# Two-layer streaming encoder on one core: sums of squares on GpSimd, halved last units, a late quarter turned ahead, and diagonal products in the last norm

## The chip, the cores and the metric

The kernel runs on one core of one Trainium2 chip. The metric is the device time of one execution in microseconds (us). The runs shown are three executions; a further execution was taken with the hardware profiler, and all rows come from that one.

A core has TensorE (PE; its weight loads are listed as PEld), VectorE (DVE), ScalarE (ACT), GpSimd (POOL) and SyncE (SP, which here issues nearly all transfers). TensorE's clock has two levels, 2.4 and 1.2 GHz; the profile gives the granted clock as a share of the higher one, so 0.50 is 1.2 GHz.

## The reference

One sequence of 256 tokens and 2048 channels goes through two layers, all in float32. With `mod = silu(c) @ w_mod + b_mod` cut into shift_m, scale_m, gate_m, shift_f, scale_f and gate_f, each layer computes:

```python
h = layer_norm(x) * (1 + scale_m) + shift_m
uv, q_c, kv_c, k_r, sb, sc, sh, ag = split(h @ w_in)
y_b = mla(rms_norm(q_c) @ w_uq, rms_norm(kv_c) @ w_ukv, k_r)
y = concat(y_a, y_b, y_c, y_d) @ w_out
x = layer_norm(ALPHA * x + (1 + gate_m) * y, g, b)
h = layer_norm(x) * (1 + scale_f) + shift_f
gate, val = split(h @ w_up)
x = layer_norm(ALPHA * x + (1 + gate_f) * ((silu(conv3(gate)) * val) @ w_down), g, b)
```

y_a is a chunked gMLP, y_c a short gated convolution, y_d a convolution of width 31 with its own norm. The latent attention y_b needs the sum of squares over 384 columns of q_c and over 256 columns of kv_c for each token. A product keeps float32 precision by one of two routes: "exact" float32 products, which the profile shows as two records each, or a split of each operand into a high and a low part, with three products hi*hi, lo*hi and hi*lo.

## The kernel before

The residual x stays on the core in two token tiles of 128 rows (t = 0 and 1). Weights are streamed. `weights` (L423) loads 1 MB into a ring of four raw tiles and makes the two parts, ScalarE the cast (L458), VectorE the difference (L459). `stream` (L402) is the order of all work: it issues a load, flushes the products appended before (`pending`), appends this load's products, and calls `pump`. So the products of one load stand in TensorE's program behind the next load. The order of instructions on one engine is fixed when the program is built, by a planner that may put ready work ahead of work that is not.

**The modulation in the background.** `mod_stream` (L324) is a generator: each of its units loads a piece of w_mod into the same raw ring and accumulates it on VectorE (`mod_step` L245, lines L249 and L251). `pump` (L376) adds the phase's rate (RATES, L35) to a credit and draws one unit for each whole credit. `settle` (L300) turns a finished accumulator into the modulation's columns with small products into ps_mod, a copy, and ScalarE's or VectorE's step on it. Of layer 0's SHIFT_F and SCALE_F the last quarter (k tiles 12 to 15, LATE_KT) is held back: four times one unit of each, eight units, drawn by the phase `first` (six loads) and, what is left, by `needs` in `late`.

**The first group of the feed-forward.** `first_group` (L616) makes the first 512 columns of `h @ w_up` with exact weights, quarter by quarter as the norm's k tiles become ready. `to_hT` (L587) normalises a quarter of one token tile (xn, ScalarE), turns it by four transposes on TensorE (L597) into one PSUM bank and applies scale and shift from there (ScalarE for t = 0, VectorE L608 for t = 1). In layer 0 three quarters are done at once; the fourth, `rest` (L655), waits for the held-back modulation. `ffn_up` (L1366) runs six other loads in the meantime (gv 0, gg 0, gv 1, gg 1, gv 2, gg 2) and puts `late` (L1401) behind them: needs, rest, gated_first.

**The output projections.** `out_proj` (L666) serves o (w_out) and d (w_down) in both layers, so o0, d0, o1, d1. The last 512 columns keep their last four loads back (`tail`) and then take token tile 0's products first, tile 1's second. `finish_bank` (L699) reads the PSUM bank: yg (L704), x (L707), batch statistics (L710). Then comes the norm: `second` (L729) for tile 0 where another layer part follows, `norm` (L770) otherwise: two VectorE passes per 512 columns, L777 (centre and gain) and L780 (rstd and bias); at the program's end (then is None) a store of each quarter (L784), 256 KB.

**The attention.** `mix_b` (L1028) squares five blocks of 128 x 256 on ScalarE (L1050), scales q (L1054) and sums the squares over the partitions with products against ones into ps_ss: ten products, 20 records. From these come rr (`power`, GpSimd, L114), diagonal tiles dgB and ps_rkv. The C products (C_c) of the same projection stand around them.

## Time and profile before

| what | before |
|---|---|
| runs, us | 2276.4, 2278.2, 2282.6 (median 2278.2) |
| profiled execution, its own time | 2274.61 us |
| its span | 2272.8 us |
| TensorE busy | 2229.4 us (98%) |
| VectorE busy | 1780.5 us (78%) |
| ScalarE busy | 1107.0 us (49%) |
| GpSimd busy | 35.1 us (2%) |
| memory traffic | 605.19 MB, mean 266 GB/s |

The span runs from the first to the last instruction of the profiled execution; its own time is 1.8 us more. All starts below are us from the span's start. Records of TensorE overlap, and their ends are modelled, so the cost of a run of products is read from start to start. "[0.52 <-PE ps_xT L597]" behind a row means that its engine idled 0.52 us before it, and what released it.

### The profile page before, as it was taken

How to read it: one execution, taken by the hardware profiler on the slowest of the kernel's cores; microseconds unless marked ns; L12 is line 12 of the kernel's file. 1: busy time of each engine (PE TensorE's matmuls, PEld its weight loads, DVE VectorE, ACT ScalarE, POOL GpSimd, SP SyncE). 2: the span in 40 equal slices, each digit the busy share in tenths (PEclk: the TensorE clock that was granted, in tenths of full speed). 3: DMA queues.
4: the chain of work that ended last, by engine and by line, in shares of the span. 5: the costliest groups of instructions: out<-in, count | busy, mean ns of one | idle time of the engine just before them, and what ended most of it. 6: DMA issues, size and time to landing. Idle time of an engine off the chain costs nothing.

```text
span 2272.8 us, 31376 instructions
## 1 busy us (share of the span) xinstructions
PE 2229.4 (98%) x12311; PEld 1919.6 (84%) x12311; DVE 1780.5 (78%) x2195; ACT 1107.0 (49%) x1652; POOL 35.1 (2%) x65
## 2 busy tenths in 40 slices
PE   7999999999999999999999999999999999999998
PEld 5788886788888888888789999889888888888886
DVE  5778988878888888989977899887775565565776
ACT  3356642354455444544554434545544454454553
POOL 0011000000000000000000000000000000000000
PEclk9999999999999999999999999999999999999999
DMA  9999699778888888899867677775675555555554
GB/s 350 388 371 361 254 327 360 245 275 315 310 313 313 309 317 325 300 343 328 296 235 251 203 242 248 281 269 178 232 258 185 190 187 198 185 187 197 187 188 148
DMA packets 228717, 605.19 MB, mean 266 GB/s; under 512 B 14661, under 2 KB 27189, under 8 KB 210901
## 3 DMA queue, kind: packets, MB, share of 16 engines
q1 hardware_dynamic: 227784, 602.30, 74.2%
q8 instruction: 96, 1.57, 0.3%
q0 software_dynamic: 784, 0.90, 0.1%
q14 instruction: 53, 0.43, 0.0%
HBM read 601.05 MB, written 2.10 MB: 265 GB/s over the span
## 4 chain that ended last, share of the span: by engine, by line
PE 89%; DVE 6%; DMA 2%; issue 1%; ACT 1%; POOL 0%; SPq 0%; DVEq 0%; ACTq 0%; POOLq 0%
PE g_c L83 22%; PE v_c L83 22%; PE d L83 19%; PE o L83 7%; PE C_c L83 4%; PE D_c L83 4%; PE B_c L83 2%; DVE wlo L459 1%; PE U_c L83 1%; PE E L83 1%; PE E_c L83 1%; PE U L83 1%; PE V L83 1%; DMA wmod<-in_w_mod_dram 1%; DVE macc L251 1%
## 5 line engine op out<-in xcount | busy, mean ns | idle before, releaser
L458 ACT CAST whi<-wraw 128x1024 fp32r<-128x1024 f32 (+1 forms) x632 | 643.3, 1043 | 751.6 <-PE g_c L83 221.7
L459 DVE TENSOR_TENSOR wlo<-wraw,whi 128x1024 fp32r<-128x1024 f32 (+1 forms) x632 | 750.3, 1213 | 302.7 <-ACT whi L458 283.1
L83 PE MATMUL d<-whi,a 128*128 128x512 f32 x1344 | 388.5, 390 | 2.3 <-ACT whi L458 2.3
L251 DVE SCALAR_TENSOR_TENSOR macc<-wmod,cact,macc 128x2048 f32<-128x2048 f32 (+2 forms) x174 | 353.7, 2033 | 24.4 <-DMA wmod<-in_w_mod_dram 23.7
L83 PE MATMUL v_c<-hT,whi 128*128 128x512 f32 (+1 forms) x1456 | 343.1, 383 | 0.0
L83 PE MATMUL g_c<-hT,whi 128*128 128x512 f32 (+1 forms) x1344 | 313.3, 380 | 0.0
L83 PEld LDWEIGHTS v_c<-hT,whi 128*128 128x128 f32 x1456 | 264.5, 189 | 48.5
L83 PEld LDWEIGHTS d<-whi,a 128*128 128x128 f32 x1344 | 251.7, 188 | 55.7 <-ACT whi L458 3.5
L83 PEld LDWEIGHTS g_c<-hT,whi 128*128 128x128 f32 x1344 | 243.4, 189 | 43.2
L83 PE MATMUL d<-wlo,a 128*128 128x512 f32 x672 | 233.5, 390 | 1.7 <-DVE wlo L459 1.7
L83 PE MATMUL v_c<-hT,wlo 128*128 128x256 f32 x1400 | 190.7, 283 | 0.0
L83 PEld LDWEIGHTS v_c<-hT,wlo 128*128 128x128 f32 x1400 | 183.1, 191 | 6.6
L83 PE MATMUL g_c<-hT,wlo 128*128 128x256 f32 x1280 | 175.8, 283 | 0.0
L83 PEld LDWEIGHTS g_c<-hT,wlo 128*128 128x128 f32 x1280 | 168.2, 191 | 5.9
L83 PEld LDWEIGHTS d<-wlo,a 128*128 128x128 f32 x672 | 126.1, 188 | 30.5 <-DVE wlo L459 4.3
L478 ACT CAST a<-g 128x512 fp32r<-128x512 f32 x132 | 80.7, 619 | 81.9 <-PE d L83 80.2
L83 PE MATMUL o<-whi,a 128*128 128x512 f32 x384 | 110.5, 392 | 0.5 <-ACT whi L458 0.5
L479 DVE TENSOR_TENSOR a<-g,a 128x512 fp32r<-128x512 f32 x132 | 87.5, 683 | 5.4 <-ACT a L478 5.4
L251 DVE SCALAR_TENSOR_TENSOR qacc<-wmod,cact,qacc 128x1024 f32<-128x1024 f32 (+1 forms) x75 | 80.3, 1071 | 11.6 <-DMA wmod<-in_w_mod_dram 9.2
L83 PEld LDWEIGHTS o<-whi,a 128*128 128x128 f32 x384 | 72.0, 188 | 16.9 <-ACT whi L458 1.3
L83 PE MATMUL D_c<-hT,whi 128*128 128x256 f32 x432 | 83.0, 292 | 2.2 <-ACT hT L478 1.6
L1381 DVE SCALAR_TENSOR_TENSOR u<-g,pf,u 128x254 f32<-128x254 f32 (+1 forms) x176 | 73.5, 478 | 0.0
(370 smaller groups left out, 2618.1 us busy)
## 6 DMA issues: line engine op xcount, KB each, us to landing
wraw<-in_ffn_w_up_dram SPq DMA_DIRECT2D x168, 1024.0 KB, 4.9
wmod<-in_w_mod_dram SPq DMA_DIRECT2D x134, 1024.0 KB, 6.0
wraw<-in_ffn_w_down_dram SPq DMA_DIRECT2D x88, 1024.0 KB, 5.3
wraw<-in_w_in_dram SPq DMA_DIRECT2D x33, 1024.0 KB, 7.5
wmod<-in_w_mod_dram SPq DMA_DIRECT2D x64, 512.0 KB, 9.2
wraw<-in_w_out_dram SPq DMA_DIRECT2D x26, 1024.0 KB, 5.2
wmod<-in_w_mod_dram SPq DMA_DIRECT2D x32, 768.0 KB, 8.0
wexact<-in_w_in_dram SPq DMA_DIRECT2D x46, 512.0 KB, 7.4
```

Source lines behind the costliest of these rows:

```text
L83: pe.matmul(o, lhsT, rhs, start=start, stop=stop, skip_group_check=True)
L251: i = dve.scalar_tensor_tensor(out=acc, in0=w, scalar=col, in1=acc, op0=ALU.mult, op1=ALU.add)
L458: act.copy(hi[:, :m], r)
L459: i = dve.tensor_tensor(out=lo[:, :m], in0=r, in1=hi[:, :m].bitcast(F32), op=ALU.subtract)
L478: act.copy(hi, src)
L479: dve.tensor_tensor(out=lo, in0=src, in1=hi.bitcast(F32), op=ALU.subtract)
L1381: dve.scalar_tensor_tensor(out=u[:, sh:], in0=x[:, : S - sh], scalar=col(k, j), in1=u[:, sh:], op0=ALU.mult, op1=ALU.add)
```

## The change

It has five parts.

1. RATES: `first` is 1.335 instead of 1.2.
2. The late quarter: `mod_stream` settles SHIFT_F as soon as its last unit is drawn. `first_group` returns two more functions: `scaled` makes the normalised last quarter of both token tiles (xn), `turn_raw` transposes it and copies it into hF without scale and shift. `ffn_up` appends them behind gv 1 and gg 1. `rest` then applies scale and shift in place, two of four blocks on ScalarE and two on VectorE, and runs the products.
3. In `out_proj` the products of the last load are made in two column halves for the token tile whose norm comes first (tile 0; tile 1 at the end of the program), and `finish` takes yg and x in the same halves.
4. At the program's end `last_rows` takes the place of `norm` for token tile 1: for quarters 0 and 1 the second pass becomes a product of a diagonal tile (rstd) with x on top of the bias in PSUM, and a ScalarE copy; quarters 2 and 3 keep VectorE's two passes.
5. In `mix_b` GpSimd adds the squares (three adds of 128 x 256), so that four products, eight records, are left.

```diff
-    dict(B=1.634, C=1.9, out=1.7, first=1.2, up=0.68, down=0.83),
+    dict(B=1.634, C=1.9, out=1.7, first=1.335, up=0.68, down=0.83),
...
                             late.append((0, v, acc, LATE_KT, KT))
+                            if v == SHIFT_F:
+                                settle(len(late) - 1)
...
+        def scaled():
+            for t in range(2):
+                raw[t] = tmp_tile("xn")
+                ident_act(raw[t], X[t][:, 3 * 512 :], r[t][:, 0:1], r[t][:, 1:2])
+
+        def turn_raw():
+            for t in range(2):
+                ps = ms_tile("ps_xT")
+                for j in range(4):
+                    pe.transpose(ps[:, j * P : (j + 1) * P], raw[t][:, j * P : (j + 1) * P], ident)
+                act.copy(hF[3][:, :, t * P : (t + 1) * P], ps.rearrange("p (j t) -> p j t", j=4))
+
         def rest():
-            for q in range(quarters, 4):
-                for t in range(2):
-                    turned(t, q)
-                products(q, 0, S, False, q == 3)
-                splits(q)
...
+            for j in range(4):
+                h, sc, sh = hF[3][:, j, :], MOD[(l, m_scale, 12 + j)], MOD[(l, m_shift, 12 + j)]
+                if j % 2 == 0:
+                    ident_act(h, h, sc, sh)
+                else:
+                    dve.tensor_scalar(out=h, in0=h, scalar1=sc, scalar2=sh, op0=ALU.mult, op1=ALU.add)
+            products(3, 0, S, False, True)
+            splits(3)
...
+        first_ready = 1 if then is None else 0
+
+        def halved(t, item, ps, h):
+            parts, acts = item
+            cols = slice(h * 256, (h + 1) * 256)
+            for k, (hi, lo) in enumerate(parts):
+                ahi, alo = acts[k]
+                end = k == len(parts) - 1
+                pairs = [(ahi, hi)] if lo is None else [(ahi, hi), (ahi, lo), (alo, hi)]
+                for i, (x, y) in enumerate(pairs):
+                    mm(ps[t][0][:, cols], x[:, t * P : (t + 1) * P], y[:, cols], False, end and i == len(pairs) - 1)
...
         def finish(t, ps, c0):
+            if t == first_ready:
+                for h in range(2):
+                    y = tmp_tile("yg")[:, :256]
+                    lo = c0 + h * 256
+                    xs = X[t][:, lo : lo + 256]
+                    dve.tensor_tensor(
+                        out=y, in0=ps[t][0][:, h * 256 : (h + 1) * 256], in1=box["gate"][:, lo : lo + 256], op=ALU.mult
+                    )
+                    dve.scalar_tensor_tensor(out=xs, in0=xs, scalar=ALPHA, in1=y, op0=ALU.mult, op1=ALU.add)
+                dve.bn_stats(out=stats[t][:, c0 // 512, :], in_=X[t][:, c0 : c0 + 512])
+                return
...
+        def last_rows(mv, r):
...
+            ps = {}
+            for q in (0, 1):
+                ps[q] = acc_tile(f"{name}_z{q}")
+                mm(ps[q], ident, gb[1][:, cut[q]], True, False)
+            centred(0)
+            centred(1)
+            dg = tmp_tile("dgB")[:, 0:P]
+            dve.tensor_scalar(out=dg, in0=ident, scalar1=r[:, 0:1], scalar2=None, op0=ALU.mult)
+            for q in (0, 1):
+                mm(ps[q], dg, X[1][:, cut[q]], False, True)
+                act.copy(X[1][:, cut[q]], ps[q])
+                store(q)
+            for q in (2, 3):
+                centred(q)
...
+                store(q)
...
                     for item, u in state["tail"]:
-                        products(t, item, state["ps"], u, nk)
+                        if last and t == first_ready and u == units - 1:
+                            for h in range(2):
+                                halved(t, item, state["ps"], h)
+                        else:
+                            products(t, item, state["ps"], u, nk)
...
+            for into, other in ((0, 1), (3, 4), (0, 2)):
+                pool.tensor_tensor(out=sqs[into], in0=sqs[into], in1=sqs[other], op=ALU.add)
             ps = ms_tile("ps_ss")
             for t in range(2):
-                for j in range(3):
-                    mm(ps[:, t : t + 1], sqs[j][:, t * P : (t + 1) * P], ones[:, 0:1], j == 0, j == 2)
                 for j in range(2):
-                    mm(ps[:, 2 + t : 3 + t], sqs[3 + j][:, t * P : (t + 1) * P], ones[:, 0:1], j == 0, j == 1)
+                    mm(ps[:, 2 * j + t : 2 * j + t + 1], sqs[3 * j][:, t * P : (t + 1) * P], ones[:, 0:1], True, True)
...
             for g, u in ((gv, 0), (gg, 0), (gv, 1), (gg, 1), (gv, 2), (gg, 2)):
                 stream(lambda: g[1](u), lambda item, g=g, u=u: g[2](item, u))
+                if (g, u) == (gv, 1):
+                    pending.append(scaled)
+                elif (g, u) == (gg, 1):
+                    pending.append(turn_raw)
             pending.append(late)
```

## Rows read from the trace of the kernel before

**Rows 1.** Page of the profile: the chain that ended last, by engine.

```profile
PE 89%; DVE 6%; DMA 2%; issue 1%; ACT 1%; POOL 0%; SPq 0%; DVEq 0%; ACTq 0%; POOLq 0%
```

**Rows 2.** Chain of waits, 410 to 512: start us, us, what.

```profile
470.91 5.76 PE g_c L83 x48
476.67 2.14 PE ps_mod L83 x20
...
479.13 0.82 ACT xn L86
```

**Rows 3.** TensorE's timeline, 474 to 515: start us, us, engine, line, operation.

```profile
479.99 1.39 PE L597 MATMUL ps_xT<-cst,xn 128*128 128x128 f32 x8 [1.20 <-ACT xn L86]
482.00 10.12 PE L83 MATMUL g_c<-hF,wexact 128*128 128x256 f32 x32 [0.62 <-ACT hF L86]
```

**Rows 4.** Chain of waits, 222 to 240.

```profile
233.30 5.38 PE ps_qn L83 x24
```

**Rows 5.** Windows: busy us (instructions) of PE, PEld, DVE, ACT, POOL, clock, DMA share, GB/s.

```profile
482.00:488.00 6.00, 6.00 (x14) 4.83 (x15) 5.55 (x7) 2.17 (x4) 0.00 (x0) 0.50 0.71 274
```

**Rows 6.** Groups by line, shapes apart.

```profile
L86 ACT ACTIVATE hF<-hF,mod,mod 128x256 f32<-128x256 f32 x8 | 4.5, 594 | 0.0
```

**Rows 7.** TensorE's timeline, 1518 to 1522.

```profile
1519.63 1.36 PE L597 MATMUL ps_xT<-cst,xn 128*128 128x128 f32 x8 [2.01 <-ACT xn L86]
1520.84 1.38 PE L83 MATMUL g_c<-hF,wexact 128*128 128x128 f32 x10
```

**Rows 8.** ScalarE's timeline, 460 to 490.

```profile
467.94 1.05 ACT L458 CAST whi<-wraw 128x1024 fp32r<-128x1024 f32 x1 [1.83 <-PE v_c L83]
```

**Rows 9.** VectorE's timeline, 462 to 515.

```profile
471.03 0.74 DVE L251 SCALAR_TENSOR_TENSOR macc<-wmod,cact,macc 128x512 f32<-128x512 f32 x1
...
473.37 2.33 DVE L251 SCALAR_TENSOR_TENSOR macc<-wmod,cact,macc 128x512 f32<-128x512 f32 x3 [0.24 <-DMA wmod<-in_w_mod_dram]
```

**Rows 10.** Chain of waits, 1310 to 1340.

```profile
1327.07 1.23 PE ps_ss L83 x12
```

**Rows 11.** GpSimd's timeline, 190 to 235.

```profile
201.11 0.31 POOL L1091 MEMSET rope<- 64x256 f32 x1 [4.69 <-PE ps_mix L83]
...
228.43 1.01 POOL L114 TENSOR_TENSOR rr<-rr,mhalf 128x4 f32<-128x4 f32 x1 [26.65 <-DVE rr L1072]
```

**Rows 12.** TensorE's timeline, 210 to 240.

```profile
222.52 9.30 PE L83 MATMUL C_c<-hF,wexact 128*128 128x256 f32 x28
```

**Rows 13.** Windows, 214 to 395, columns as in rows 5.

```profile
222.00:228.00 6.00, 6.00 (x17) 4.92 (x17) 5.95 (x9) 5.84 (x15) 0.00 (x0) 0.50 1.00 415
314.00:395.00 81.00, 79.75 (x309) 55.24 (x308) 68.30 (x69) 23.98 (x30) 0.00 (x0) 1.00 0.95 350
```

**Rows 14.** Timeline of all engines, 1190.8 to 1192.5.

```profile
1191.17 0.60 PE L597 MATMUL ps_xT<-cst,xn 128*128 128x128 f32 x4
...
1191.81 0.81 ACT L86 ACTIVATE hF<-ps_xT,mod,mod 128x128 f32<-128x128 f32 x2 [0.52 <-PE ps_xT L597]
```

**Rows 15.** VectorE: groups by line, shapes apart, and the timeline from 2255.

```profile
L1439 DVE TENSOR_TENSOR second<-v_c,second 128x256 f32<-128x256 f32 x84 | 33.2, 418 | 26.1 <-ACT second L1425 25.6
...
2261.50 0.69 DVE L704 TENSOR_TENSOR yg<-d,gate 128x512 f32<-128x512 f32 x1 [2.95 <-PE d L83]
```

**Rows 16.** Timeline of all engines, 2261 to 2274.

```profile
2265.37 1.41 DVE L780 SCALAR_TENSOR_TENSOR x<-x,rs_d1p,gb 128x512 f32<-128x512 f32 x2
2266.14 3.65 SPq L784 DMA_DIRECT2D out_dram<-x  x4
...
2268.02 1.41 DVE L780 SCALAR_TENSOR_TENSOR x<-x,rs_d1p,gb 128x512 f32<-128x512 f32 x2
```

**Rows 17.** Windows, the end, columns as in rows 5.

```profile
2267.00:2272.00 5.00, 0.00 (x0) 0.00 (x0) 2.43 (x4) 0.00 (x0) 0.00 (x0) 0.50 0.54 207
```

**Rows 18.** VectorE's timeline and the window 1110 to 1131, columns as in rows 5.

```profile
1118.22 1.28 DVE L249 TENSOR_SCALAR macc<-wmod,cact 128x2048 f32<-128x2048 f32 x1
...
1110.00:1131.00 21.00, 18.92 (x82) 13.40 (x80) 20.60 (x28) 11.66 (x16) 0.00 (x0) 1.00 0.75 262
```

More of the change, by code (lines that the diff above doesn't have):

```diff
@@ L653, in first_group @@
             splits(q)
-        def rest():
-            for q in range(quarters, 4):
-                for t in range(2):
-                    turned(t, q)
-                products(q, 0, S, False, q == 3)
-                splits(q)
-        return cps, rest
+        raw = {}
+        def scaled():
[8 more added lines that the diff above has]
+                act.copy(hF[3][:, :, t * P : (t + 1) * P], ps.rearrange("p (j t) -> p j t", j=4))
+        def rest():
+            if quarters == 4:
+                return
[7 more added lines that the diff above has]
+            splits(3)
+        return cps, rest, scaled, turn_raw
     CHUNKS = ((0, 1024), (1024, 512), (1536, 512))
@@ L695, in finish @@
         def finish(t, ps, c0):
+            if t == first_ready:
[8 more added lines that the diff above has]
+                dve.bn_stats(out=stats[t][:, c0 // 512, :], in_=X[t][:, c0 : c0 + 512])
+                return
             for i in range(len(ps[t])):
@@ L768, in second, with centred, store @@
             box[t] = r
+        def last_rows(mv, r):
+            gb = box["gb"]
+            cut = [slice(q * 512, (q + 1) * 512) for q in range(4)]
+            def centred(q):
+                xs = X[1][:, cut[q]]
+                dve.scalar_tensor_tensor(
+                    out=xs, in0=xs, scalar=mv[:, 0:1], in1=gb[0][:, cut[q]], op0=ALU.subtract, op1=ALU.mult
+                )
+            def store(q):
+                nc.sync.dma_start(out=out[0, P:S, cut[q]], in_=X[1][:, cut[q]])
+            ps = {}
[12 more added lines that the diff above has]
+                centred(q)
+                dve.scalar_tensor_tensor(
+                    out=X[1][:, cut[q]],
+                    in0=X[1][:, cut[q]],
+                    scalar=r[:, 0:1],
+                    in1=gb[1][:, cut[q]],
+                    op0=ALU.mult,
+                    op1=ALU.add,
+                )
+                store(q)
         def norm(t):
@@ L772, in norm @@
             mv, r = rstd_of(stats[t], f"{name}p{t}", False)
+            if then is None and t == 1:
+                last_rows(mv, r)
+                return
             st2 = new_stats(f"{name}q{t}")
@@ L833, in out_proj, with done @@
                 stream(lambda: load(u), lambda item, u=u, unit=unit: unit(item, u), bg, not last)
-            def done(state=state, c0=c0, nk=nk, last=last):
+            def done(state=state, c0=c0, nk=nk, last=last, units=units):
                 if c0 == 0:
@@ L1391, in gated_first @@
                 background.append(lambda j=j0 + j: gate_conv(j))
-        cps, rest = first_group(w, 0, f"g{l}0", l, SHIFT_F, SCALE_F, LATE_KT // 4 if l == 0 else 4)
+        cps, rest, scaled, turn_raw = first_group(w, 0, f"g{l}0", l, SHIFT_F, SCALE_F, LATE_KT // 4 if l == 0 else 4)
         if l == 0:
```

## The prediction

> **What bounds the kernel now.** I read the page's chain of waits first [rows 1]: TensorE carries 89% of it, VectorE 6%. So a microsecond of another engine counts only where TensorE stands still for it, and TensorE's own time counts where it runs. Five places are touched; for each I then read the chain there, the timeline of the engines and the granted clock.
>
> The sum is made against the profiled execution, 2274.6 us. The median of the runs shown is 2278.2, 3.6 above it, and that offset is added at the end.
>
> **Part 1, the late quarter.** The reader is to see in the chain [rows 2] that products follow one another up to 476.67, and that then 20 small ps_mod products and xn come, and in TensorE's timeline [rows 3] that the transposes and 32 products of the last quarter close the row at 492.12: 15.45 us. The 32 take 10.12, although an exact 256-column record costs 5.38/24 = 0.224 elsewhere [rows 4], so 7.2 for 32. The difference of 2.9 is the clock: 0.50 granted from 482 to 488 [rows 5], that is 1.2 GHz, after a stretch in which TensorE had only ps_mod, waits of 1.20 and 0.62, and transposes [rows 3].
>
> After the change half of ps_mod (1.07 of 2.14) and the transposes (1.39) lie ahead of gg2's products. They still cost TensorE 2.46, for they run between products. Behind gg2 remain 1.07 of ps_mod, then the scale's ScalarE step (0.28) and the first in-place modulation. The nearest row of that shape costs 0.59 [rows 6]; with semaphores about 0.95. Then 32 records, 7.2 if the clock stays. That it stays I take from a nearer row than this one: at layer 1's first norm TensorE waited 2.01 before its transposes [rows 7], and the products behind kept their speed, ten in 1.38 [rows 7]. The low stretch here shrinks from 5.3 to 2.0. Sum: 2.46 + 1.07 + 0.95 + 7.2 = 11.7, a gain of 3.75; a third of a us off for waits gives **-3.4**. If the clock falls all the same, the gain is 3.75 - 2.9 = 0.8.
>
> What is moved: two xn on ScalarE (0.82 each [rows 2]) and two copies out of PSUM (under 0.82 each by the same row) fall into the idle 1.83 that lies ahead of each cast [rows 8]. If that cover were gone, a cast would be late by 0.8 at most. VectorE's two in-place steps take the place of four of L608. The rate 1.335 draws 0.404 + 6 x 1.335 = 8.4, so eight units and not 0.404 + 6 x 1.2 = 7.6, seven; on SP's queue the last SHIFT_F load now stands ahead of gg2's weights and the last SCALE_F load, before issued on demand, ahead of gv3's. I cost that at nothing while gg2 lands before its first cast at 467.94 [rows 8]. The settle puts SHIFT_F's ps_mod right behind gg1's products and the transposes in program order, at about 465.15 + 1.39 = 466.5. In the trace SHIFT_F's last step ends at 471.77, and four SCALE_F steps wait for their transfer after that [rows 9]. One load slot earlier the steps should end by about 467 to 469, so the wait lies between 0 and 5.3; I take a third of a us, since the order on an engine is laid by a planner that can put gv2's products in between.
>
> **Part 2, the squares.** Three GpSimd adds replace 12 of 20 ps_ss records per layer. In layer 1 the last 12 cost 1.23 in the chain [rows 10], about 1.4 with the interleaving. The adds come behind the fifth square, on a queue that is empty (GpSimd idles 26.65 before its power step [rows 11]); the trace has no add of 128 x 256 on GpSimd. The rows on either side are a memset of 64 x 256, 0.31, and a power on 128 x 4, 1.01 [rows 11]; I take 0.9, nearer the two-operand row, and two in series are 1.8. If the planner leaves C_c products ahead of ps_ss, as it did with four of them, they cover most of it; what stands behind ps_ss on TensorE, the rest of C_c and by way of rr ps_rkv, waits for what is not covered. I leave 0.5 uncovered: **-0.9**, between -1.4 (all covered) and +0.4 (nothing is).
>
> The Trainium skill, "GPSIMD Engine Reference", section 3.1 Elementwise, speaks against this step: a GpSimd tensor_tensor needs about 2.6 cycles per element, roughly twice VectorE's time for 2048 fp32. An estimate from its 4497 ns, scaled to 256 elements, is 0.56 us an add, cheaper than I take it, and the sum would be lower by at most 0.3; no row here has such an add.
>
> In layer 0 the stall is larger. TensorE's 28 C_c records behind the same 12 take 9.30 [rows 12] where 28 x 0.224 = 6.3 were due; the clock was 0.50 from 222 to 228 [rows 13]. So 1.4 - 0.5 + 2.9 = 3.8 if the tiny products no longer bring the clock down. Behind it lies the o stage, where TensorE is busy for 79.75 of 81 us, but the DMA share is 0.95 at 350 GB/s [rows 13]: time saved ahead of it comes back partly as waiting for weights. I take 60%: **-2.3**, between 0 and -3.8.
>
> **Part 3, the halves.** In o0, d0 and o1 the last unit's three records per k tile become six of half the columns for token tile 0, and finish does yg and x in halves. The gain would be VectorE's first half under TensorE's second. But both halves lie in one PSUM bank, and a reader of one block waits for every write to its bank: hF's modulation of the first block begins at 1191.81, after all four transposes, with 0.52 idle put down to them [rows 14]. So I let them run one after the other. A 256-wide VectorE step costs 0.418 and a 512-wide one 0.69 [rows 15]: 4 x 0.418 + 0.69 against 3 x 0.69 is +0.25 with gaps; TensorE takes 24 records of 0.120 (48 in 5.76 [rows 2]) for 12 of 0.227, +0.16. At o0 the path to the norm runs through tile 1 as well, so +0.1 there, +0.4 at d0, +0.4 at o1: **+0.9**. If they overlap it is about -0.4 at each instead.
>
> **Part 4, the end.** Now VectorE runs from 2261.50 [rows 15] through norm(1) to 2269.43; stores go out from 2266.14 [rows 16]. After: finish +0.25 and TensorE +0.16, so rstd, which L780 takes up at 2265.37 now, is there at about 2265.6; two centred steps (1.41) have run by then. The diagonal (an estimate of 0.25, 128 columns against 0.418 for 256), a product of two records at 512 columns (0.9, four times the 0.224 of [rows 4]) and a ScalarE copy (0.6, the row of [rows 6]) put the first store at about 2267.8, the second at 2268.4. VectorE's quarters 2 and 3 are done at 2267.5 and 2268.9, against 2268.7 and 2269.43. SP issues in order, so quarter 2's store waits for quarter 1's. All four now fall into 1.1 us instead of 3.4; four stores take 0.54 of 5 us of the transfer engines [rows 17], 0.7 each, so one after the other they cannot be through before 2267.8 + 4 x 0.7 = 2270.6 and a fixed delay; the last one alone, at 2269.43 + 0.7 = 2270.1 and the same delay, sets the end now. The difference is 0.5, less for a transfer that overlaps its neighbour: **+0.3**, from -0.75 (the last store decides alone) to +0.6 (the clock at half speed during the diagonal products).
>
> **Part 5, what the rate moves.** Credit of 0.41 and not 0.60 is left after the six loads; 78 loads at 0.68 (53.04) carry 0.45 and not 0.64 into the down projection of layer 0, which then draws 27 units (0.45 + 33 x 0.83 = 27.84) and not 28 (0.64 + 27.39 = 28.03). One step of 1.28 leaves a stretch in which VectorE is busy for 20.60 of 21 us and TensorE for 18.92 [rows 18]: **-0.6**, from 0 to -1.28.
>
> **Sum.** -3.4 - 0.9 - 2.3 + 0.9 + 0.3 - 0.6 = -6.0: 2268.6 profiled, **2272.2 us** as a median.
>
> **The rivals.** *The halves overlap* (chance 0.1): for it, the two halves share no element; against it [rows 14]. Three times 0.4 gained in place of 0.9 lost is 2.1, and 0.65 more at the last output: 2269.5. *All of layer 0's time arrives* (0.2): 1.5 more, 2270.7; for it, TensorE is busy nearly throughout the o stage; against it the 0.95 DMA share of [rows 13]. *Layer 0's clock falls anyway, or GpSimd is slow* (0.15): part 2 gives 1.5 instead of 3.2: 2273.9. For it, TensorE still has eight tiny products there and waits for the adds ahead of them; against it, [rows 7]. *The other side* (0.1): SHIFT_F's ps_mod stands in TensorE's queue before its steps are done. TensorE then waits up to 5.3 ahead of gv2's products, all behind it waits too, and the clock falls for 2.9 as it did in [rows 5]: part 1 turns from -3.4 to +4.4 and the time is 2280.0. It decides from the point where the wait passes the gain, 3.75 us. That the change does not do what it says is no rival of weight: each edit has its instructions.
>
> **How the numbers follow.** My forecast has 0.45. Nothing below 0.3% of 2278.2, 6.8 us, can be told from no change, so faster means under 2271.4 and slower over 2285.0. The forecast lies 0.8 above the lower bound and puts about a third of its chance below; the two fast rivals lie below or at it for the most: faster 0.40, same 0.53, slower 0.07 (the other side with layer 0's gain lost besides, and gg2's weights late). The range reaches down to 2265: both fast rivals at once give 2268.0, and the runs shown lie between 1.8 under and 4.4 over their median. Upwards, the clock lost in the late quarter (2.9) together with the slow case of part 2 (1.7) gives 2276.8, and with the same scatter I go to 2279; of the other side's 0.1 most lies outside.
>
> **What would show it.** Part 1: 32 g_c records in about 7.2, the clock at 1.00 behind gg2, ps_mod of 10 records twice. Part 2: eight ps_ss records per layer, C_c at 0.22 each in layer 0. Part 3: yg of 256 columns beginning only after TensorE's last record. Part 4: four stores within about 1.1 us. Part 5: one L249 step less before d0's last products. It is wrong if TensorE waits ahead of gv2's products, if the clock is 0.50 after 482, or if yg's first half runs while TensorE writes the second.

## The result and the profile after

The changed kernel takes 2281.52 us as a median of 20 runs, against 2277.6 us for 20 runs of the kernel before; the ratio is 1.0017, 95% interval 1.001 to 1.0024. So it is slower by 3.9 us: the interval leaves out 1, but the difference is less than the 0.3% that the prediction asks of one. The forecast was 2272.2 us, range 2265 to 2279. The profiled execution took 2280.76 us, the one of before 2274.61. Its page has:

```profile
span 2279.0 us, 31448 instructions
...
PE 2232.7 (98%) x12339; PEld 1922.8 (84%) x12339; DVE 1783.0 (78%) x2200; ACT 1109.1 (49%) x1654; POOL 44.3 (2%) x71
```

GpSimd's busy time rose by 9.2 us with six more instructions, 1.5 us each. The rest of the page hardly moves, so the stages have to be read one by one. In layer 0's attention part, TensorE's timeline of the changed kernel (start us, us, operation, and in brackets the idle time before it and who ended it) answers to [rows 12]:

```profile
221.35 0.38 PE L83 MATMUL ps_ss<-onesR,sqB 128*128 128x1 f32 x2 [3.38 <-POOL sqB L1150]
...
222.98 1.44 PE L83 MATMUL ps_ss<-onesR,sqB 128*128 128x1 f32 x6 [0.28 <-POOL sqB L1150]
224.28 8.86 PE L83 MATMUL C_c<-hF,wexact 128*128 128x256 f32 x28
```

Before, the products of the small sums began at 218.6; now the first waits 3.38 us for a GpSimd add, and the 28 C_c products behind the rest still take 8.86 (9.30 before). GpSimd's and VectorE's timelines of the same stretch:

```profile
216.94 1.62 POOL L1150 TENSOR_TENSOR sqB<-sqB 128x256 f32<-128x256 f32 x1 [21.01 <-ACT sqB L1137]
218.65 4.28 POOL L1150 TENSOR_TENSOR sqB<-sqB,sqB 128x256 f32<-128x256 f32 x2
...
228.77 1.02 POOL L114 TENSOR_TENSOR rr<-rr,mhalf 128x4 f32<-128x4 f32 x1 [5.12 <-DVE rr L1159]
```

```profile
216.79 1.20 DVE L1000 TENSOR_TENSOR convD<-convD,prodD 128x992 f32<-128x992 f32 x1
217.89 2.82 DVE L251 SCALAR_TENSOR_TENSOR macc<-wmod,cact,macc 128x2048 f32<-128x2048 f32 x1
220.64 1.70 DVE L1000 TENSOR_TENSOR convD<-convD,prodD 128x988 f32<-128x988 f32 x1
...
224.28 1.16 DVE L1000 TENSOR_TENSOR convD<-convD,prodD 128x980 f32<-128x980 f32 x1
```

The first add runs from 216.94 to 218.56. VectorE's convD, in progress since 216.79, ends at 217.99, and 0.57 later the add is done. The next two start at 218.65 and take 4.28 together. VectorE's modulation step runs until 220.71 and its next convD until 222.34; the second of the two adds is done at 222.93, 0.59 after that. TensorE confirms the ends: its last six small products, which wait for this add, start at 222.98. VectorE pays as well: 2.82 and 1.70, where the same operations take 2.35 and 1.17 a little earlier or later.

The late quarter, TensorE's timeline [rows 3] and one window (columns as in rows 5):

```profile
466.88 1.04 PE L668 MATMUL ps_xT<-cst,xn 128*128 128x128 f32 x8
...
471.07 1.18 PE L83 MATMUL ps_mod<-onesR,macc 128*128 128x1 f32 x8 [1.11 <-DVE macc L251]
...
483.66 1.03 PE L83 MATMUL ps_mod<-onesR,macc 128*128 128x1 f32 x8
...
485.68 7.17 PE L83 MATMUL g_c<-hF,wexact 128*128 128x256 f32 x32 [0.31 <-ACT hF L86]
```

```profile
472.00:474.00 2.00, 2.00 (x11) 2.00 (x11) 0.90 (x2) 0.16 (x1) 0.00 (x0) 0.50 1.04 402
```

The 32 products of the quarter now take 7.17, and 0.31 us of wait is left ahead of them (10.12 and 0.62 before). But SHIFT_F's ps_mod stands in the midst of gv2's products, TensorE waits 1.11 us there for VectorE's last step, and the clock behind it is 0.50.

Layer 1's first norm [rows 7], first TensorE, then the window behind it, then VectorE's finish of token tile 0:

```profile
1522.83 1.82 PE L599 MATMUL ps_xT<-cst,xn 128*128 128x128 f32 x8 [4.01 <-ACT xn L86]
1524.44 4.75 PE L83 MATMUL g_c<-hF,wexact 128*128 128x128 f32 x32
```

```profile
1523.00:1527.00 4.00, 4.00 (x22) 3.75 (x22) 3.90 (x9) 3.75 (x10) 0.98 (x1) 0.57 1.04 398
```

```profile
1511.80 0.76 DVE L733 TENSOR_TENSOR yg<-o,gate 128x256 f32<-128x256 f32 x2 [2.73 <-PE o L83]
1512.47 0.75 DVE L736 SCALAR_TENSOR_TENSOR x<-x,yg 128x256 f32<-128x256 f32 x2
1513.26 0.69 DVE L737 BATCH_NORM_STATS2 st_o<-x 128x6 f32<-128x512 f32 x1
1513.98 0.26 DVE L576 BATCH_NORM_AGGREGATE mv_o1p<-st_o 128x2 f32<-128x24 f32 x1
```

TensorE's wait has grown from 2.01 to 4.01 us, and the granted clock behind it is 0.57 where it was 1.00 from 1520 to 1527 in the profile of before. The finish takes 2.18 us from the first yg to the aggregate, as before (1508.60 to 1510.78): the two 256-column steps together are 0.76. What is longer is the wait ahead of it, 2.73 us.

The end, the diagonal products on TensorE and the stores on SP, which answer to [rows 16]:

```profile
2270.68 3.65 PE L83 MATMUL d_z<-x,dgB 128*128 128x512 f32 x4 [2.53 <-DVE dgB L833]
```

```profile
2273.41 2.39 SPq L824 DMA_DIRECT2D out_dram<-x  x4
```

Four records take 3.65 us. The window 2271 to 2274 has a granted clock of 0.50. From the last d product's start to the end of the span it is 12.8 us, 11.7 before.

### The profile page after: what moved, and what is told of

The parts are those of the page before. It is cut to its first block, busy times and chain, and to the rows that moved or that the text cites. A ratio compares the mean times of both kernels' runs of the same rounds, so it can differ in the third digit from the quotient of the medians.

```text
span 2279.0 us, 31448 instructions
## 1 busy us (share of the span) xinstructions
PE 2232.7 (98%) x12339; PEld 1922.8 (84%) x12339; DVE 1783.0 (78%) x2200; ACT 1109.1 (49%) x1654; POOL 44.3 (2%) x71
## 5 line engine op out<-in xcount | busy, mean ns | idle before, releaser
L83 PE MATMUL d<-whi,a 128*128 128x512 f32 (+1 forms) x1360 | 389.1, 387 | 0.6 <-ACT whi L460 0.6
L83 PE MATMUL d<-wlo,a 128*128 128x512 f32 (+1 forms) x680 | 235.3, 388 | 2.0 <-DVE wlo L461 1.9
L83 PEld LDWEIGHTS d<-wlo,a 128*128 128x128 f32 x680 | 127.7, 188 | 31.1 <-DVE wlo L461 5.2
L480 ACT CAST a<-g 128x512 fp32r<-128x512 f32 x132 | 80.6, 618 | 71.7 <-PE d L83 70.1
L83 PE MATMUL o<-whi,a 128*128 128x512 f32 (+1 forms) x392 | 110.7, 388 | 0.2 <-ACT whi L460 0.2
L1468 DVE SCALAR_TENSOR_TENSOR u<-g,pf,u 128x254 f32<-128x254 f32 (+1 forms) x176 | 73.8, 481 | 2.2 <-ACT u L86 2.2
```

The source lines that it names most:

```text
L83: pe.matmul(o, lhsT, rhs, start=start, stop=stop, skip_group_check=True)
L480: act.copy(hi, src)
L1468: dve.scalar_tensor_tensor(out=u[:, sh:], in0=x[:, : S - sh], scalar=col(k, j), in1=u[:, sh:], op0=ALU.mult, op1=ALU.add)
```

## The experiments

Three theories stood against each other for the loss: the GpSimd adds, the column halves, and the diagonal products. A fourth came up with the second set of runs: that the rate itself moved something in layer 1. For each run the ratio to the kernel before on the same chip is given with its interval. These intervals are 1.6 to 3 us to either side, so the places in the traces carry the verdicts; but each run has one trace, and the two of the kernel before differ by 4.2 us in their spans. The table has, from the starts of products in each trace: (A) the span's start to layer 0's first ps_qn, and (G) the end of that stretch alone, from the last B_c product (the projection that q_c and kv_c come from), which leaves out how the program started; (B) the first transposes after o0 to the first product behind the late quarter; (C) layer 0's down projection, first to last product; (D) o1's last product to layer 1's first transposes; (F) o1's first product to the first v_c product of layer 1's up projection, so D with the products on either side of it; (E) the last d product to the end. All in us.

```
run                        ratio (95% interval)       A      G      B      C     D      F     E
before, first profile      -                       233.2   14.9   75.3  251.0   2.4  124.7  11.7
c1_before_again            0.9993 (0.9984-1.0002)  231.1   14.1   75.0  252.7   2.4  126.2  11.7
e5_rate_only               0.9988 (0.9979-0.9998)  231.9   13.6   74.5  249.5   4.0  127.5  11.7
changed, first profile     1.0017 (1.0010-1.0024)  234.6   17.0   73.8  249.9   4.4  129.2  12.8
c2_after_again             1.0015 (1.0004-1.0026)  235.4   17.9   71.4  250.0   4.4  127.9  11.8
e1_no_squares              0.9994 (0.9984-1.0003)  232.4   14.3   71.9  250.3   4.4  129.3  11.8
e2_no_halves               0.9997 (0.9985-1.0009)  233.8   16.9   71.7  249.5   4.0  127.4  12.3
e3_no_last_rows            1.0001 (0.9990-1.0012)  236.5   17.8   71.5  250.1   4.4  128.3  11.6
e4_no_settle               1.0009 (1.0000-1.0018)  234.2   16.8   73.2  252.2   4.4  128.3  12.5
e10_halves_by_pair         1.0010 (1.0000-1.0020)  234.3   17.1   74.8  249.6   4.0  127.7  12.7
e7_adds_beside             1.0007 (0.9996-1.0017)  233.7   16.2   74.7  253.1   2.4  126.8  11.7
e6_late_settle             0.9964 (0.9952-0.9976)  230.5   13.6   71.0  249.5   4.0  127.2  11.7
e8_late_settle_squares     0.9989 (0.9980-0.9998)  234.8   16.4   72.7  249.5   4.0  127.7  11.7
e9_late_settle_phase       0.9960 (0.9947-0.9974)  230.6   13.6   72.7  249.5   2.4  126.8  11.7
```

**Controls.** Both kernels were run once more, unchanged.

> The kernel before, unchanged, as a control of the measurement: both theories expect a ratio of 1 within its interval. It tells how far a stage differs between two profiled executions of one kernel: theory A (what the four variants share moved layer 1's last weights) expects 10 us or more from the end of the last split of o1 to TensorE's last product there, 2 us of wait ahead of the transposes and no low clock at that place again; rival B (that place scatters from run to run) expects 9 us, a wait of 3 to 4 us and a low clock, as in the four variants.

> The changed kernel, unchanged, beside the others on one chip. Both theories expect the ratio of the record, 1.001 to 1.0024. Theory A: the same four places again (ps_ss waits over 3 us in layer 0, a wait and a low clock in the midst of gv2's products, 4 us ahead of layer 1's transposes, 12.5 us from the last product to the end). Rival B: some of them, the wait in gv2's products above all, are chance of one execution and are missing.

The control's ratio is 1 within its interval, and D is 2.4 again, so that wait is a property of the kernel (theory A). But the clock behind it is as rival B has it (window, columns as in rows 5):

```profile
1523.00:1526.50 3.50, 3.50 (x19) 3.42 (x20) 3.43 (x8) 3.50 (x10) 0.99 (x1) 0.59 1.04 390
```

It fell behind a wait of 2.00 us. Of all fourteen executions only the first profile of the kernel before kept 1.00 there; in the others the clock is 0.50 to 0.71 in the 4 us behind the start of the transposes, whether the wait was 2 or 4 us. So the low clock at o1 is no work of the change. The control differs from the first profile in layer 0's attention part as well:

```profile
220.77 6.29 PE L83 MATMUL C_c<-hF,wexact 128*128 128x256 f32 x28
228.91 0.67 PE L83 MATMUL ps_rkv<-dgB,onesR 128*128 128x256 f32 x2 [1.85 <-DVE dgB L1079]
```

With all 20 small products ahead of them the 28 C_c products took 6.29 us, not the 9.30 of [rows 12], and TensorE then waited 1.85 us for VectorE's dgB. The changed kernel repeats A and D; in B the wait in gv2's products is only 0.23 us in c2 and the clock stays, so the 73.8 of the first profile was its worse case; E was 11.8. Both theories hold in part.

**The adds.** Taken out of the changed kernel:

```diff
-            for into, other in ((0, 1), (3, 4), (0, 2)):
-                pool.tensor_tensor(out=sqs[into], in0=sqs[into], in1=sqs[other], op=ALU.add)
...
-                for j in range(2):
-                    mm(ps[:, 2 * j + t : 2 * j + t + 1], sqs[3 * j][:, t * P : (t + 1) * P], ones[:, 0:1], True, True)
+                for j in range(3):
+                    mm(ps[:, t : t + 1], sqs[j][:, t * P : (t + 1) * P], ones[:, 0:1], j == 0, j == 2)
...
```

> The changed kernel without the GpSimd adds (ten products into ps_ss again, all else kept). Theory A, the adds cost at layer 0: TensorE no longer waits 3.38 us for them, the VectorE steps beside them go back from 1.70 to about 1.2 us, and the stage's products run 2 us earlier than in the changed kernel; in layer 1 nothing is lost or won by the end of the projection. In all 2 us less than the changed kernel, about +2 against before. Rival B: the o stage behind it is fed by transfers, so the 2 us come back there and the time stays that of the changed kernel (+4 against before).

A fell from 234.6 and 235.4 to 232.4, and the convD steps take 1.18 again: theory A for the place. The total fell by more than its 2 us, from 1.0015 and 1.0017 to 0.9994, some 5 us with an interval of 2 to 3. TensorE's timeline adds something the prediction had not seen:

```profile
220.51 1.50 PE L83 MATMUL ps_ss<-onesR,sqB 128*128 128x1 f32 x12 [0.29 <-ACT sqB L1137]
221.87 6.29 PE L83 MATMUL C_c<-hF,wexact 128*128 128x256 f32 x28
230.01 0.67 PE L83 MATMUL ps_rkv<-dgB,onesR 128*128 128x256 f32 x2 [1.85 <-DVE dgB L1166]
```

Here too the clock stayed up (1.00 from 221 to 228), and the 28 C_c products took 6.29. But 1.85 us of the gain turned into a wait for VectorE's dgB, as in the control. By G the low clock of [rows 13] had cost 0.8 us against the control, 1.3 against e5_rate_only, and not 2.9.

The adds by themselves: the kernel before, with three adds into a half tile that is never read, so that no data ties TensorE to them.

```diff
+            for one, other in ((0, 1), (3, 4), (0, 2)):
+                pool.tensor_tensor(out=sq[2][:, S:], in0=sqs[one], in1=sqs[other], op=ALU.add)
             ps = ms_tile("ps_ss")
```

> The kernel before with the three GpSimd adds run beside it into a free half tile that nothing reads; ps_ss keeps its ten products. Theory A, GpSimd and VectorE hinder each other: in layer 0 each add takes 1.5 us or more and the VectorE steps that overlap it are 0.4 to 0.5 us longer than elsewhere, although no data binds them; TensorE does not wait, so the projection is at most 1 us longer. Rival B, the adds are slow by themselves and what cost time in the changed kernel was only that TensorE waited for them: VectorE's steps keep 1.2 and 2.35 us.

GpSimd's timeline and then VectorE's:

```profile
216.87 1.63 POOL L1063 TENSOR_TENSOR sqB<-sqB 128x256 f32<-128x256 f32 x1 [21.31 <-DVE macc L251]
220.03 2.83 POOL L1063 TENSOR_TENSOR sqB<-sqB,sqB 128x256 f32<-128x256 f32 x2 [1.54 <-ACT sqB L1050]
```

```profile
216.72 1.20 DVE L913 TENSOR_TENSOR convD<-convD,prodD 128x992 f32<-128x992 f32 x1
217.82 2.83 DVE L251 SCALAR_TENSOR_TENSOR macc<-wmod,cact,macc 128x2048 f32<-128x2048 f32 x1
220.57 1.70 DVE L913 TENSOR_TENSOR convD<-convD,prodD 128x988 f32<-128x988 f32 x1
```

Theory A for the lengths: 1.63 for the first add, and VectorE's 2.83 and 1.70, nearly the numbers of the changed kernel although nothing depends on the adds. Theory A missed that TensorE loses all the same; G is 16.2, against 14.9 and 14.1 in the two profiles of the kernel before:

```profile
221.31 6.29 PE L83 MATMUL C_c<-hF,wexact 128*128 128x256 f32 x28
230.57 1.19 PE L83 MATMUL ps_rkv<-dgB,onesR 128*128 128x256 f32 x2 [2.98 <-DVE dgB L1081]
```

Counted from the last B_c product, VectorE is done with dgB after 11.8 us in all six executions without adds, and after 12.9 in all eight with them, this one included. So 1.1 us of the loss is VectorE's own work made longer, whether anything waits for the adds or not. Most of the rest is the clock: in the seven executions in which TensorE waits for the adds, the 28 C_c products behind them take 7.8 to 9.3 us; in this one, and in five of the six without adds, they take 6.29. Here the clock fell later, behind the 2.98 us of waiting: ps_rkv takes 1.19 where it is 0.67 in the control.

And on top of the best version found (below), the adds alone, with the same edit as in the change:

> The late quarter turned ahead with SHIFT_F settled behind gv2's products (ratio 0.9964 of before), and the GpSimd adds with eight records in ps_ss on top; no halves, the old norm at the end. Theory A: the adds alone cost 3 us up to layer 0's first attention product (235 us instead of 231 to 232) and give nothing back in layer 1, so the ratio is 0.9975 to 0.998. Rival B: what the changed kernel lost lay in the halves and the last norm, and the ratio stays at 0.9964 or falls.

A rose from 230.5 to 234.8, G from 13.6 to 16.4, and the ratio from 0.9964 to 0.9989: theory A again, though the total rose by more than its 3 us (5.7, from two ratios whose intervals are 2 to 3 us to either side). In the profiled execution the clock fell in the late quarter besides, and B is 1.7 longer.

**The halves.** Both conditions set to False, so that products and finish are as before:

```diff
-            if t == first_ready:
+            if False:
...
-                        if last and t == first_ready and u == units - 1:
+                        if False:
```

> The changed kernel without the column halves (last unit and finish as before, for o0, d0, o1 and d1). Theory A, the halves make tile 0 end later at o1, because column half 0 needs the last weights before half 1 may start: TensorE's wait ahead of layer 1's first transposes goes back from 4.0 to 2 us, the clock stays at 1.00 there, and the products behind it come 3 us earlier; in all about 3 us less than the changed kernel, +1 against before. Rival B, the wait comes from the last weights, which landed 1 us later: the wait stays above 3 us, the clock falls, and at most 1 us is won.

D fell only from 4.4 to 4.0, and VectorE's wait for tile 0's last product from 2.73 to 1.84 us. So the halves explain 0.4 us of D and no more; for the remaining 1.6 theory A falls and rival B stands: the last weights come late. But the total fell by more than rival B's 1 us: from 1.0015 and 1.0017 to 0.9997, which is 4 to 5 us with intervals of 2 to 3. By the places the halves cost 0.6 in C, 1.2 in F (the means of the runs with halves in this order, e4 aside in C, against those without, all at the new rate) and 0.8 in the last down projection. Why halves cost at all, the next run tells; the order of the products was changed and nothing else:

```diff
-                            for h in range(2):
-                                halved(t, item, state["ps"], h)
+                            for k0 in range(0, nk, 2):
+                                for h in range(2):
+                                    halved(t, item, state["ps"], h, k0)
```

> The changed kernel with the halved products in another order: both column halves of the first two k tiles, then both halves of the last two. Theory A, half 0 first needs the last weights before half 1 may begin: from the end of o1's last split to yg it takes 1.9 us, as without halves, and not 2.5 to 2.7 as in the changed kernel, and the wait ahead of layer 1's transposes is 0.5 us shorter. Rival B: 2.5 us or more stay, since 256-column products are slower than their count says.

VectorE's first yg in this run and in e2_no_halves:

```profile
1510.40 0.76 DVE L733 TENSOR_TENSOR yg<-o,gate 128x256 f32<-128x256 f32 x2 [1.99 <-PE o L83]
```

```profile
1506.59 0.69 DVE L747 TENSOR_TENSOR yg<-o,gate 128x512 f32<-128x512 f32 x1 [1.84 <-PE o L83]
```

1.99 us against 1.84 here and 1.74 to 2.09 in all runs without halves, and 2.46 to 2.73 in those with half 0 first; D is 4.0 again: theory A. When the last split arrives, the order by pairs has only the third and fourth k tile of the unit left, as without halves; with half 0 first, those of half 0 and all of half 1 are left.

**The rate.** The remaining 1.6 us of D are in all variants of the changed kernel, so the rate, which they all share, was tried alone on the kernel before (first 1.335 instead of 1.2).

> The kernel before with the rate 1.335 alone. Theory A: one modulation step of 1.28 us leaves layer 0's down projection, which takes 0.6 to 1.5 us less from its first to its last product, and the last weights of o1 come 1 us later for TensorE with a wait of 3 to 4 us there; together about 0. Rival B: the down projection is as long as before (250.9 us) and o1 as before (wait of 2 us), since the moved unit meets no bound.

D is 4.0 and C is 249.5: theory A on both places. Its total of about 0 is too careful: the ratio is 0.9988, 2.7 us less with an interval that just leaves out 1, so the rate as a whole did not lose time. SP's timeline ahead of o1's last loads, first of the kernel before, then of this run:

```profile
1459.76 0.37 SPq L444 DMA_DIRECT2D wraw<-in_w_out_dram  x1
1464.83 0.34 SPq L352 DMA_DIRECT2D wmod<-in_w_mod_dram  x1
1467.10 5.24 SPq L444 DMA_DIRECT2D wraw<-in_w_out_dram  x2
1473.11 0.34 SPq L352 DMA_DIRECT2D wmod<-in_w_mod_dram  x1
1477.77 0.37 SPq L444 DMA_DIRECT2D wraw<-in_w_out_dram  x1
1481.83 0.34 SPq L716 DMA_DIRECT2D gb<-in_post_mix_g_dram  x1
```

```profile
1456.25 5.80 SPq L444 DMA_DIRECT2D wraw<-in_w_out_dram  x2
1463.95 0.34 SPq L352 DMA_DIRECT2D wmod<-in_w_mod_dram  x1
1467.13 0.37 SPq L444 DMA_DIRECT2D wraw<-in_w_out_dram  x1
1472.67 0.34 SPq L352 DMA_DIRECT2D wmod<-in_w_mod_dram  x1
1476.12 0.37 SPq L444 DMA_DIRECT2D wraw<-in_w_out_dram  x1
1478.39 0.34 SPq L716 DMA_DIRECT2D gb<-in_post_mix_g_dram  x1
```

The same loads, but the modulation pieces (wmod) stand elsewhere between o1's weights: of the last four wraw loads ahead of gb, before, the second and third follow each other without a piece between them; here it is the first and second. The credit explains it: 0.034 goes from the down projection into layer 1 before, 0.844 with one unit fewer here, and at the end of B it is 0.834 against 0.644, so units are drawn at other loads of C, E and o. Counted from o1's first product, the last split ends after 79.4 us before and after 80.6 here, while TensorE's last product stands at 89.8 in both: from the split to that product there are 10.4 us left before and 9.1 here. The last weights come 1.2 us later, and TensorE waits for what hangs on them. The test of that: D's rate set so that the credit is 0.434 after D's eight loads, as before.

```diff
-    dict(D=0.8, U=0, V=0, B=0.3, C=0.6, E=0.6, out=0.6, up=0.3, down=0.7),
+    dict(D=0.82375, U=0, V=0, B=0.3, C=0.6, E=0.6, out=0.6, up=0.3, down=0.7),
```

> The late quarter turned ahead with SHIFT_F settled behind gv2's products, and layer 1's rate D at 0.82375 instead of 0.8, so that from the end of D's eight loads the units are drawn at the same loads as in the kernel before (credit 0.434). Theory A, the order of the background loads among o1's weights sets TensorE's wait there: the wait ahead of layer 1's first transposes goes back from 4.0 to 2.4 us, 10 us and more lie between the last split and TensorE's last product, and 1.5 to 3 us are won: ratio 0.995 to 0.996. Rival B: the wait stays at 4 us, since it hangs on other things than that order, and the ratio stays at 0.9964.

The first transposes of layer 1 in e5_rate_only and in this run:

```profile
1517.31 1.94 PE L597 MATMUL ps_xT<-cst,xn 128*128 128x128 f32 x8 [3.59 <-ACT xn L86]
```

```profile
1515.38 1.80 PE L597 MATMUL ps_xT<-cst,xn 128*128 128x128 f32 x8 [2.00 <-ACT xn L86]
```

The wait is 2.00 again, and 10.4 us lie between the last split and TensorE's last product: theory A for the mechanism. Its 1.5 to 3 us are not shown: 0.9960 and 0.9964 can't be told apart, and the clock fell behind the 2 us wait in this execution. F is 126.8, as in e7_adds_beside, which has the old order of loads too; the control has 126.2, and the four runs with the new order and no halves have 127.2 to 127.7. So in time the order costs about 0.8 us, half of what the wait grew by.

**The late quarter.** Without the early settle:

> The changed kernel without the early settle of SHIFT_F (both ps_mod groups behind gg2 again, transposes still ahead). Theory A: the wait of 1.1 us for VectorE in the midst of gv2's products and the fall of the clock behind it go, some 2.8 us; behind gg2 stand 2.14 of ps_mod and about 0.9 of waits, the clock stays, and the late quarter ends about 2 us sooner than in the changed kernel. Rival B: the 20 small products behind gg2 bring the clock to 0.50 as in the kernel before, the 32 products take 9 to 10 us and the late quarter ends no sooner than in the changed kernel.

The wait in gv2's products goes, but 20 small products stand behind gg2 again, and the 32 products behind them took 8.86 us; the clock is 0.76 from 483 to 490. B is 73.2, between the 73.8 and the 71.4 of the two profiles of the changed kernel: rival B, though milder than in the kernel before. Better is a place in between: rate, transposes and in-place modulation as in the change, without adds, halves and last_rows, and with SHIFT_F settled one load later.

```diff
-                            if v == SHIFT_F:
-                                settle(len(late) - 1)
...
+                elif (g, u) == (gv, 2):
+                    pending.append(needs(l, SHIFT_F))
```

> The kernel before with the rate and the late quarter turned ahead, but SHIFT_F settled behind gv2's products and not behind gg1's; no GpSimd adds, no halves, the old norm at the end. Theory A: nothing waits in the midst of gv2's products, the clock stays at 1.00 through the late quarter, and from layer 0's first norm to the end of the late quarter it takes 71.5 us against 75.3 before and 73.8 in the changed kernel; the total is 2 to 4 us under before. Rival B: the clock falls at another place of the late quarter, or the time is lost at o1 again, and the total is that of before within 1.5 us.

```profile
468.56 1.03 PE L83 MATMUL ps_mod<-onesR,macc 128*128 128x1 f32 x8
...
477.44 7.17 PE L83 MATMUL g_c<-hF,wexact 128*128 128x256 f32 x32 [0.31 <-ACT hF L86]
```

Nothing waits ahead of ps_mod, the 32 products take 7.17, B is 71.0, and the median is 2272.17 us: a ratio of 0.9964, less than that of either kernel. Theory A for the place; its total, 2 to 4 us, is exceeded: 7.1 us, of which B has 4.3 and the rate alone 2.7, partly the same, so a part of it stays open. The clock still falls in this quarter in other executions of the same code: e8 and e9 have 8.86 for the 32 products.

**The end.** With `norm` for token tile 1 (the three lines that call last_rows taken out):

> The changed kernel with the old norm for token tile 1 at the end (halves kept). Theory A: the diagonal products run at half the clock (0.9 us each of four) and set the stores; with VectorE alone the time from the last product to the end is 11.3 us as before and not 12.6, so 1.2 to 1.4 us less than the changed kernel. Rival B: the end is set by the four transfers, and the time from the last product to the end does not change by over 0.3 us.

E is 11.6, against 11.8 to 12.8 with last_rows. The difference is the clock; c2_after_again's diagonal products and stores:

```profile
2269.23 1.98 PE L83 MATMUL d_z<-x,dgB 128*128 128x512 f32 x4 [2.54 <-DVE dgB L833]
```

```profile
2271.01 1.80 SPq L824 DMA_DIRECT2D out_dram<-x  x4
```

At 2.4 GHz four records take 1.98 us and E is 11.8, no better than VectorE alone; at 1.2 GHz they take 3.65 and E is 12.8. The other four lie between: 2.43, 3.02, 3.37 and 3.48 us for the four records, and 11.8, 12.3, 12.5 and 12.7 for E. Theory A holds for the first profile of the changed kernel, rival B where the clock stays.

## Why the prediction was wrong

**Part 1** was right in mechanism and size: 3.4 us less forecast, and 3.4 to 3.9 less measured in B wherever the early settle stood and the clock stayed (71.4 to 71.9 against 75.3), of which the rate alone gives 0.8 (74.5 in e5). The step "I take a third of a us" for SHIFT_F's ps_mod was measured at 0.17 to 1.74 us, and in two of the six executions with the early settle (1.11 and 1.74 us of wait) the clock fell behind it and took 2 to 3 us back. That is the rival of the other side, in a smaller size than its 5.3 us.

**Part 2** is the step that failed: "I take 0.9, nearer the two-operand row", with C_c products to cover it. It was forecast at -0.9 and -2.3. In layer 0 the adds took 1.62, 2.65 and 1.67, one after the other, and the first small product stood ahead of the C_c products and waited 3.38 for them. The mean of A is 234.8 for the seven executions in which the adds are waited for and 231.6 for the six without adds, so layer 0 alone is +3.2 (+3.1 by G). Layer 1 gives nothing back: from its first U_c product to the first of o1 it is 240.8 and 241.2 us in the two profiles of the changed kernel, 239.9 and 241.4 in the two of before. Neither of [rows 11] is an add that starts beside a VectorE step in progress: the memset reads nothing, and the power step began while VectorE was idle. Beside VectorE's long two-input steps an add is not done until the step in progress is over. The slow rival had the wait, but with a loss of 1.7 against the forecast where 6.3 were measured: it left out that VectorE's steps grow too, and that the clock falls behind the wait.

Nor was there 2.9 us to win from the clock. The condition "if the tiny products no longer bring the clock down" has the wrong cause: the control kept the clock with all 20 of them. And dgB sets that stretch next, 1.85 us later. The question asked of every other stall, what is late next, was not asked there. Both readings of the clock came from one execution, and both were its exceptions: the low clock of [rows 13], one in six executions without adds, and the clock that stayed behind the wait of [rows 7], one in fourteen. So part 1 came out right in size, but the row that it took the steady clock from does not carry it: that is luck.

The estimate from the Trainium skill, 0.56 us an add, is what is left of an add once VectorE's step is done: 0.57 and 0.59 above. The Trainium skill, "SBUF — State Buffer", section Who interferes with whom, says why: VectorE with two inputs from SBUF and a reading GpSimd instruction share one port pair, and the second to start is blocked until the first is through. The ends of the adds above agree; that it is the ports, no run here shows by itself. In layer 1, where VectorE's steps are short (0.45), the adds took 0.94, 0.78 and 0.80.

**Part 3**, forecast at +0.9, was too small, and by another mechanism: not the finish (2.18 us in both forms; the +0.25 for it is not there), but the order in which the last weights are used. D has the forecast +0.4 at o1, but F has +1.2. For d0 about 0.6 can be read from C (249.9 to 250.3 with half 0 first, e4 aside; 249.6 in e10; 249.5 without, at the new rate). The last down projection, from layer 1's first v_c product on, is 709.3 to 710.5 with halves and 709.0 to 709.2 without. That makes about +2.6 in place of the +0.9, counting d0, o1 and this projection. Whether yg of one half could run while TensorE writes the other half of the bank was not tried; in the changed kernel's profile both halves began after tile 0's last product.

**Part 4**: forecast +0.3, up to +0.6 with the clock at half speed; measured 0 to +1.1. The bound for half speed was set too low: the four records took 3.65 us instead of 1.98, and both stores wait for them.

**Part 5** was right at its place: one modulation step fewer in layer 0's down projection (26 and not 27), TensorE's idle time there 2.8 us instead of 4.25, and C 1.5 less at the new rate without halves, a little past the bound of -1.28. In the control and in e7 the clock fell there besides (a mean of 0.99 over the stretch), and C is 252.7 and 253.1; e4 has 252.2 at the new rate, with 4.3 of idle time, and why is open. But the credit was followed no further than layer 0. Its phase in layer 1 costs 1.6 us of wait at o1, about 0.8 in time.

Taken together, the means of the two profiles of each kernel differ by +3.0 in G, -2.5 in B, -1.9 in C, +3.2 in F, +1.0 in the last down projection, +0.6 in E and -0.5 in all the rest: +2.9. The 3.9 us measured are near it, but two executions of a kernel differ by as much, so this does not fix the shares. Of F's +3.2 some 0.8 is the clock that only the first profile of before kept; what decides in which executions the clock falls in the late quarter stays open.

## What to carry over

An add on GpSimd is not free because GpSimd is idle: price it by the VectorE step that may be in progress, here 1.2 to 2.4 us, ask what waits for the result, and add what it takes from VectorE, here half a us a step, even where nothing waits. Before a sum rests on the clock of a stretch, look at a second execution of the same kernel. A rate that paces background loads has a phase; after a change of it, follow the credit to the end of the program and compare the order of loads at each place where TensorE waits for the last weights. If the last weights arrive just in time, cut a unit along its weights and not across them.

## What was not expected

The clock behind one and the same code falls in some executions and not in others: the late quarter's 32 products, with 10 small products behind gg2, took 7.17 us in e6 and 8.86 in e8 and e9. With 20 small products there they took 8.72 to 10.12 in all five executions; with 10, they took 7.17 in seven of nine. And a VectorE step is lengthened by about half a us when a GpSimd add that reads two tiles overlaps it (2.35 to 2.82, 1.17 to 1.70), with no data between them.
